# Weight chunks at a cycle of eight distances from the activations, in a one-core hybrid attention block

## The chip, the core and the metric

The kernel runs on one core of one Trainium2 chip. A core has a matrix engine (TensorE, PE in the profile; its weight loads stand apart as PEld), a vector engine (DVE), a scalar engine (ACT), a general engine (POOL) and SyncE (SP), whose queue starts the transfers between main memory and the on-chip memory SBUF. Matrix products land in PSUM. The metric is the device time of one execution of the whole program in microseconds (us), as a median over runs.

## The reference

One layer of a transformer block on a sequence of 256 tokens of width 2048, in float32: a half-step gated feed-forward net, attention with two groups of eight heads, an output projection, and a second half-step feed-forward net. Scales, shifts and gates come from a vector `c` through the large matrix `w_ada`.

```python
mod = jax.nn.silu(c) @ w_ada[l] + b_ada[l]
sh1, sc1, gt1, sh2, sc2, gt2, sh3, sc3, gt3 = jnp.split(mod, N_MOD, axis=-1)
f = swiglu(modulate(rms_norm(h, g_ffn1[l]), sh1, sc1), w1_gate[l], w1_up[l], w1_down[l])
h = h + 0.5 * gt1[:, None, :] * f
nrm = modulate(rms_norm(h, g_mix[l]), sh2, sc2)
q, k, v = jnp.split(nrm @ w_qkv[l], 3, axis=-1)
...
mix = jnp.concatenate([o_na, o_dil], axis=-1) @ w_o[l]
h = h + gt2[:, None, :] * mix
f = swiglu(modulate(rms_norm(h, g_ffn2[l]), sh3, sc3), w2_gate[l], w2_up[l], w2_down[l])
h = h + 0.5 * gt3[:, None, :] * f
```

The hidden width of the feed-forward nets is 5632. The q and k of each head are normalised with gains: one pair of gains for the first eight heads, another for the last eight.

## The kernel before

**Pairs of matmuls.** Weights and activations are kept in float32 accuracy by splitting each into a high part (type float32r) and a low part, the rest. `mm2` (lines 153 to 157) multiplies one 128x128 weight block with one activation tile in two matmuls: the high weights with the 512 columns "high and low activation" (line 156), then the low weights with the 256 columns of the high activation alone (line 157). In a matmul of this kind the weights are the stationary operand, loaded by an LDWEIGHTS, and the activations stream past. There are 4384 such pairs: 800 in the up-projection's first part (`pa`), 1920 in the rest of it (`pb`), 1408 in the down-projections (`pd`) and 256 in the output projection (`pso`). The q, k, v projection goes the other way round (`mm3`, line 162): the activations are stationary and the weights stream, three matmuls of 512 columns for each product, 1152 in all.

**Chunks.** All weights come as chunks of 128x1024 (512 KB, eight blocks), in the order in which they are used, listed in `srcs`. The class `W` keeps the stream: `chunk` fetches up to three chunks ahead (`AHEAD`), and for each calls `wraw` (a transfer on SP's queue into one of five `rw` buffers) and `wsplit` (lines 145 to 152): ACT copies the chunk to `hiw` (line 150), DVE subtracts it to get `low` (line 151). `hiw` and `low` have four buffers each (`LOB`), used in turn. The very first 12 chunks (`w1_s`) are used whole, without a split. Between the chunks, at a rate that `pace` sets, the stream also issues a 1 MB transfer of a `w_ada` row block and a reduction of it on DVE (line 131).

**Where tiles lie.** The pools give out addresses in the order of the first request. The activation tiles that stream in `mm2` are `nx` (normalised input), `hd` (hidden) and `ox` (attention output), each 2 KB per partition. In `wsplit` a pad `far` of 192 bytes is requested between the first `hiw` and the first `low`. In the built program every `hiw` buffer starts 64 bytes after an `nx`, `hd` or `ox` tile, counted modulo 256, and every `low` buffer starts at 0 (blocks within a chunk are 512 bytes apart). "The distance 64 and 0" below means this pair of numbers. In the q, k, v projection the same buffers give 64 for the high and 0 for the low weights.

**Order.** A scheduler orders the instructions of each engine by dependencies, except PE's in the attention stage, which are kept in the written order (`manual_schedule`). In that stage the work is cut in units of one chunk each; `at(u, fn)` puts a piece of the attention behind unit `u`. `qk_norm` multiplies q and k by their row factors and by the gains in `gq` (line 543), loaded once for all four gain rows (line 501).

The stages in order of time: start and first norm (0 to 68 us), up-projection of the first net (68 to 408), its down-projection and remaining parts (408 to 800), q, k, v with attention and the output projection (800 to 1226), the second net in the same order (up to 1580, down and the remaining parts to the end).

Of the kernel before, what the change touches and what calls it, by code (L numbers as in the profile page):

```python
# [9 lines left out]
F32 = mybir.dt.float32  # L10
F32R = mybir.dt.float32r
AF = mybir.ActivationFunctionType
ALU = mybir.AluOpType
AX = mybir.AxisListType

P = 128
# [6 lines left out]
HD = 128  # L23
EPS = 1e-6
NEG = -1e30
CW = 1024
# [21 lines left out]
LOB = 4  # L48
URGENT = 400
LINE = 16  # L50
MANUAL = {mybir.EngineType.PE}


# [10 lines left out]
def build(tc, a):  # L64
    nc = tc.nc
    with ExitStack() as ctx:
        cp = ctx.enter_context(tc.tile_pool(name="cp", bufs=1))
        wp = ctx.enter_context(tc.tile_pool(name="wp", bufs=2))
# [35 lines left out]
        cb = cp.tile([P, D], F32, name="cb")  # L104
        mods = [cp.tile([P, KT], F32, tag=f"m{j}", name=f"m{j}") for j in range(9)]
        nx = [cp.tile([P, 2, S], F32R, tag=f"nx{k}", name=f"nx{k}") for k in range(KT)]

        wide = {}
        turn = [0]
# [28 lines left out]
        def wraw(src):  # L138
            raw = wp.tile([P, CW], F32, tag="raw", bufs=RAWB, name="rw")
            nc.sync.dma_start(raw, src)  # L140
            return raw

        far = []

        def wsplit(raw):
            hi = wp.tile([P, CW], F32R, tag="whi", bufs=LOB, name="hiw")
            if not far:
                far.append(wp.tile([P, 3 * LINE], F32, tag="far", bufs=1, name="far"))
            lo = wp.tile([P, CW], F32R, tag="wlo", bufs=LOB, name="low")
            nc.scalar.copy(hi, raw)  # L150
            nc.vector.tensor_tensor(lo, raw, hi.bitcast(F32), ALU.subtract)  # L151
            return hi, lo
# [88 lines left out]
        def bg_use():  # L241
            raw, i, then = pend.pop(0)
            ada_use(raw, i)
            if then:
                then()

        def bg_step():
            i, then = bg.pop(0)
            while len(pend) >= (ARA + ARX - 1 if wide else ARA - 1):
                bg_use()  # L250
            pend.append((ada_issue(i), i, then))
# [9 lines left out]
        def ax_open():  # L261
            wide["cm"] = tc.tile_pool(name="ax", bufs=ARX)
            wide["p"] = wide["cm"].__enter__()
# [7 lines left out]
        srcs = []  # L271
        first = {}
        for nm in ("w1_s", "w1_a", "w1_b", "w1_d", "w1_c", "w1_e", "w_qkv", "w_o",
                   "w2_a", "w2_b", "w2_d", "w2_c", "w2_e"):
            first[nm] = len(srcs)
            srcs += [a[nm][c] for c in range(a[nm].shape[0])]

        class W:
            def __init__(self):
# [6 lines left out]

            def fetch(self, n):
                while self.head < n:
                    self.ready[self.head] = wraw(srcs[self.head])
                    self.head += 1  # L290

            def whole(self):
# [2 lines left out]

            def chunk(self, ahead=AHEAD):
                while self.head <= min(self.tail + ahead, len(srcs) - 1):
                    self.ready[self.head] = wsplit(wraw(srcs[self.head]))
                    self.head += 1
                    self.credit += self.rate  # L300
                    while self.credit >= 1.0 and (bg or pend):
                        self.credit -= 1.0
                        if bg:
                            bg_step()
                        else:
                            bg_use()
                self.tail += 1
                return self.ready.pop(self.tail - 1)
# [100 lines left out]
        hp = hps.enter_context(tc.tile_pool(name="hid1", bufs=F1 + 4))  # L409
        hp.tile([P, LINE], F32, tag="pad", bufs=1, name="pad1")  # L410
        ax_open()
# [36 lines left out]
        for k in range(K1):  # L448
            ws.fetch(2 * k + 2)
            bg_until((KT - 1 - k) * 2)  # L450
            for j in range(2):
                w = ws.whole()
                for b in range(8):
                    f, q = 4 * j + b // 2, b % 2
# [42 lines left out]
        hps.close()  # L497

        with tc.tile_pool(name="att", bufs=2) as ap_, tc.tile_pool(name="atc", bufs=1) as ac:
            gq = ac.tile([P, 4, HD], F32, name="gq")  # L500
            nc.sync.dma_start(gq, a["qkg"].partition_broadcast(P))
            rope = ac.tile([P, 2, 2, 32], F32, name="rope")
            nc.sync.dma_start(rope, a["rope"])
            lnc = ac.tile([P, 2, S], F32, name="lnc")
# [18 lines left out]
            def at(u, fn):  # L523
                slots.setdefault(u, []).append(fn)
# [12 lines left out]
                s_["rr"] = rstd_from(s_["ss"], HD, 8, "rq")  # L537

            def qk_norm(g, j, nm, ps, t, s_):
                gi = j + (0 if g < 2 else 2)  # L540
                xn = ap_.tile([P, 4, HD], F32, tag=f"{nm}n{t}", bufs=1, name=f"{nm}n{t}")
                for i in range(4):
                    nc.vector.scalar_tensor_tensor(
                        xn[:, i, :], ps[t][:, i * P : (i + 1) * P],
                        s_["rr"][:, t * 4 + i : t * 4 + i + 1], gq[:, gi, :], ALU.mult, ALU.mult)
                if g >= 2:
                    ra = ap_.tile([P, 4, 32], F32, tag="ra", bufs=1, name="ra")
                    rb = ap_.tile([P, 4, 32], F32, tag="rb", bufs=1, name="rb")
                    cs = rope[:, t, 0, :].unsqueeze(1).broadcast_to([P, 4, 32])
                    sn = rope[:, t, 1, :]  # L550
                    nc.vector.tensor_tensor(ra, xn[:, :, 0:32], cs, ALU.mult)
                    nc.vector.tensor_tensor(
                        rb[:, :, 0:16], xn[:, :, 16:32],
                        sn[:, 0:16].unsqueeze(1).broadcast_to([P, 4, 16]), ALU.mult)
                    nc.vector.tensor_tensor(
                        rb[:, :, 16:32], xn[:, :, 0:16],
                        sn[:, 16:32].unsqueeze(1).broadcast_to([P, 4, 16]), ALU.mult)
                    nc.vector.tensor_tensor(xn[:, :, 0:32], ra, rb, ALU.add)
                res[g, nm, t] = xn
# [7 lines left out]
            def qkv_unit(u, g, j, nm, cch, st_):  # L567
                def go(whi, wlo):
                    if cch == 0:
                        st_["ps"] = [bank(f"pq{nm}{t}") for t in range(2)]  # L570
                    ps = st_["ps"]
                    for kk in range(2):
                        k = cch * 2 + kk
                        sl = slice(kk * 512, (kk + 1) * 512)
                        for t in range(2):
                            ts_ = slice(t * P, (t + 1) * P)
                            mm3(ps[t], nx[k][:, 0, ts_], nx[k][:, 1, ts_], whi[:, sl], wlo[:, sl],
                                k == 0, k == KT - 1)
                    if cch == 7:
                        if j == 2:  # L580
                            for t in range(2):
                                at(u + 1 + t, lambda t=t: v_split(g, ps, t))
                        else:
                            at(u + 1, lambda: qk_squares(nm, ps, st_))
                            at(u + 2, lambda: qk_rstd(st_))
                            for t in range(2):
                                at(u + 3 + t // QS, lambda t=t: qk_norm(g, j, nm, ps, t, st_))
                return go
# [27 lines left out]
            def head(g, i, a0, b0, c0, d0):  # L616
# [70 lines left out]
                def fetch():  # L687
                    s_["bias"] = na_bias(hd) if g < 2 else lnc

                at(max(0, a0 - 2), fetch)  # L690
                for u, fn in ((a0, a_pe), (a0 + 1, a_ew), (b0, b_pe), (b0 + 1, b_ew1), (b0 + 2, b_ew2),
                              (c0, c_pe), (c0 + 1, c_ew), (d0, d_pe), (d0 + (0 if d0 == LAST else 1), d_ew)):
                    at(u, fn)
# [3 lines left out]
            for g in range(4):  # L697
                for j, nm in ((2, "v"), (1, "k"), (0, "q")):
                    st_ = {}
                    for cch in range(8):  # L700
                        units.append(qkv_unit(len(units), g, j, nm, cch, st_))
            LAST = len(units) + KT - 1
            for b in range(2):
                for d in range(KT):
                    units.append(wo_unit(len(units), b, d))
            ws.pace(RQ)
            with tc.manual_schedule(engines=MANUAL):
                for u in range(len(units)):
# [19 lines left out]
        hp = ctx.enter_context(tc.tile_pool(name="hid2", bufs=F1 + 4))  # L728
        hp.tile([P, LINE], F32, tag="pad", bufs=1, name="pad2")
        ax_open()  # L730
# [104 lines left out]
def _program():  # L835
    import concourse.bacc as _bacc

    nc = _bacc.Bacc("TRN2", target_bir_lowering=False, num_devices=1, dynamic_dma_scratch_size=1024)
    aps = {k: nc.dram_tensor(f"in_{k}_dram", s, F32, kind="ExternalInput").ap() for k, s in _SHAPES.items()}
    aps["out"] = nc.dram_tensor("out_0_dram", (KT, P, S), F32, kind="ExternalOutput").ap()  # L840
    with tile.TileContext(nc) as tc:
        build(tc, aps)
    return nc
# [10 lines left out]
```

## Time and profile before

| | |
|---|---|
| median of 3 runs | 1954.19 us (1942.38 to 1956.5) |
| profiled execution, its own time | 1967.14 us |
| its span | 1965.4 us |
| PE busy, weight loads busy | 1923.0 us (98%), 1659.7 us (84%) |
| DVE busy, ACT busy | 1570.2 us (80%), 906.5 us (46%) |
| mean granted TensorE clock | 0.992 |
| read from main memory | 500.09 MB, mean 256 GB/s |

How to read it: matmuls are pipelined, so that the end of one lies over the start of the next; a busy PE is therefore not a PE at its best. What counts is the time from the start of one matmul to the start of the next. In a group of matmuls that follow each other without a break, it is the stretch divided by their number.

### The profile page before, as it was taken

What the parts mean: (1) busy time and instruction counts of PE and PEld (TensorE: products, weight loads), DVE (VectorE), ACT (ScalarE), POOL (GpSimd) and SP (SyncE); (2) the same over time, 40 slices, a digit from 0 to 9 for tenths busy, and PEclk for the clock granted to TensorE, in tenths of its full rate; (3) what the DMA queues carried; (4) which work ended last, traced back from release to release, by engine and by line L of the source; (5) the groups of instructions that cost most, each with busy time, mean ns of one, the idle gap of its engine ahead of it and who ended that gap; (6) DMA issues with size and microseconds to landing.
All of it is one profiled execution on the core that took longest, in us unless ns stands there. A gap on an engine that the chain in (4) does not pass through costs nothing.

```text
span 1965.4 us, 27570 instructions
## 1 busy us (share of the span) xinstructions
PE 1923.0 (98%) x10564; PEld 1659.7 (84%) x10564; DVE 1570.2 (80%) x2122; ACT 906.5 (46%) x1333; POOL 0.7 (0%) x6
## 2 busy tenths in 40 slices
PE   7999999999999999999999999999999999999999
PEld 5878888888887888887888788888888888888888
DVE  7799999998888867989766799988899865555565
ACT  2444544443333454545554555544455443334442
POOL 0000000000000000000000000000000000000000
PEclk8999999999999999999999999999999999999999
DMA  9988888899998976698655445899976666666664
GB/s 383 360 323 296 310 304 306 301 314 337 350 336 322 330 238 202 206 336 306 219 163 165 152 134 170 317 317 334 324 263 191 192 186 189 187 188 188 188 199 133
DMA packets 120083, 503.98 MB, mean 256 GB/s; under 512 B 13328, under 2 KB 15632, under 8 KB 101520
## 3 DMA queue, kind: packets, MB, share of 16 engines
q1 hardware_dynamic: 119952, 502.24, 75.2%
q8 instruction: 82, 1.34, 0.3%
q14 instruction: 49, 0.40, 0.1%
HBM read 500.09 MB, written 2.10 MB: 256 GB/s over the span
## 4 chain that ended last, share of the span: by engine, by line
PE 86%; DVE 7%; DMA 3%; issue 2%; ACT 2%; SPq 0%; DVEq 0%; ACTq 0%
PE pb L156 22%; PE pd L156 15%; PE pb L157 11%; PE pa L156 9%; PE pd L157 7%; PE pqv L162 5%; PE pa L157 5%; PE pqk L162 4%; DVE low L151 3%; PE pa L455 2%; PE pqq L162 2%; DMA ra<-in_w_ada_dram 2%; PE pso L156 2%; DVE ra L131 1%; DMA rx<-in_w_ada_dram 1%
## 5 line engine op out<-in xcount | busy, mean ns | idle before, releaser
L150 ACT CAST hiw<-rw 128x1024 fp32r<-128x1024 f32 x644 | 674.6, 1051 | 793.3 <-PE pd L156 272.0
L151 DVE TENSOR_TENSOR low<-rw,hiw 128x1024 fp32r<-128x1024 f32 x644 | 783.2, 1222 | 246.3 <-ACT hiw L150 243.5
L156 PE MATMUL pb<-nx,hiw 128*128 128x512 f32 x1920 | 676.4, 395 | 0.0
L157 PE MATMUL pb<-nx,low 128*128 128x256 f32 x1920 | 540.1, 281 | 5.3 <-DVE low L151 5.2
L156 PE MATMUL pd<-hd,hiw 128*128 128x512 f32 x1408 | 489.9, 393 | 0.0
L156 PEld LDWEIGHTS pb<-nx,hiw 128*128 128x128 f32 x1920 | 361.1, 188 | 84.7
L157 PE MATMUL pd<-hd,low 128*128 128x256 f32 x1408 | 393.8, 280 | 1.3 <-DVE low L151 1.3
L157 PEld LDWEIGHTS pb<-nx,low 128*128 128x128 f32 x1920 | 363.0, 189 | 6.3 <-DVE low L151 6.3
L156 PEld LDWEIGHTS pd<-hd,hiw 128*128 128x128 f32 x1408 | 264.3, 188 | 59.0
L156 PE MATMUL pa<-nx,hiw 128*128 128x512 f32 x800 | 283.4, 398 | 3.6 <-ACT hiw L150 3.3
L131 DVE CUSTOM_DVE_ANT_0 ra<-ra,cb,vec 128x2048 f32<-128x2048 f32 x101 | 237.2, 2348 | 43.6 <-DMA ra<-in_w_ada_dram 42.9
L157 PEld LDWEIGHTS pd<-hd,low 128*128 128x128 f32 x1408 | 265.8, 189 | 2.2 <-DVE low L151 2.2
L157 PE MATMUL pa<-nx,low 128*128 128x256 f32 x800 | 225.4, 284 | 3.9 <-DVE low L151 3.8
L156 PEld LDWEIGHTS pa<-nx,hiw 128*128 128x128 f32 x800 | 151.1, 190 | 38.9 <-ACT hiw L150 5.2
L157 PEld LDWEIGHTS pa<-nx,low 128*128 128x128 f32 x800 | 153.0, 191 | 8.5 <-DVE low L151 7.5
L131 DVE CUSTOM_DVE_ANT_0 rx<-rx,cb,vec 128x2048 f32<-128x2048 f32 x43 | 101.0, 2348 | 20.3 <-DMA rx<-in_w_ada_dram 20.2
L156 PE MATMUL pso<-ox,hiw 128*128 128x512 f32 x256 | 92.2, 403 | 0.0
L162 PE MATMUL pqk<-hiw,nx 128*128 128x512 f32 x256 | 85.6, 399 | 0.0
L162 PE MATMUL pqq<-hiw,nx 128*128 128x512 f32 x256 | 84.4, 399 | 0.0
L162 PE MATMUL pqv<-hiw,nx 128*128 128x512 f32 x256 | 82.8, 398 | 0.3 <-ACT nx L225 0.3
L370 DVE SCALAR_TENSOR_TENSOR h<-pd,m,h 128x256 f32<-128x256 f32 x128 | 61.3, 482 | 22.5 <-PE pd L157 20.5
L157 PE MATMUL pso<-ox,low 128*128 128x256 f32 x256 | 72.1, 282 | 0.0
(133 smaller groups left out, 1513.0 us busy)
## 6 DMA issues: line engine op xcount, KB each, us to landing
ra<-in_w_ada_dram SPq DMA_DIRECT2D x101, 1024.0 KB, 7.8
rw<-in_w_b_dram SPq DMA_DIRECT2D x144, 512.0 KB, 4.7
rw<-in_w_d_dram SPq DMA_DIRECT2D x128, 512.0 KB, 4.5
rw<-in_w_a_dram SPq DMA_DIRECT2D x100, 512.0 KB, 5.0
rw<-in_w_c_dram SPq DMA_DIRECT2D x96, 512.0 KB, 4.5
rw<-in_w_qkv_dram SPq DMA_DIRECT2D x96, 512.0 KB, 4.1
rx<-in_w_ada_dram SPq DMA_DIRECT2D x43, 1024.0 KB, 7.6
rw<-in_w_e_dram SPq DMA_DIRECT2D x48, 512.0 KB, 4.2
```

The lines of the kernel that those rows point to most:

```text
L131: held(nc.vector.tensor_tensor_reduce(out=raw, in0=raw, in1=cb, scale=1.0, scalar=vec[:, BA + i : BA + i + 1], op0=ALU.mult, op1=ALU.add, ...
L150: nc.scalar.copy(hi, raw)
L151: nc.vector.tensor_tensor(lo, raw, hi.bitcast(F32), ALU.subtract)
L156: nc.tensor.matmul(out, lh, r, start=first, stop=False)
L157: nc.tensor.matmul(out[:, :S], ll, r[:, 0, :], start=False, stop=last)
L162: nc.tensor.matmul(out, l, r, start=first and i == 0, stop=last and i == 2, **kw)
L370: nc.vector.scalar_tensor_tensor(h[d], part_, g, h[d], ALU.mult, ALU.add)
L455: nc.tensor.matmul(pa[f][:, q, :], w[:, b * P : (b + 1) * P], full[k], start=k == 0 and q == 0, stop=k == K1 - 1 and q == 1, skip_group_ch ...
```

## The change

Each chunk gets a place, a pair of offsets in floats for its high and its low part. `hiw` and `low` become 64 floats longer, and the chunk lies in them at its offset. A new pad of 192 bytes behind `nx` and the loss of `far` bring the start of every `hiw` and every `low` to 0 modulo 256 from the activations, so that the offset in bytes is the distance. By the number of the chunk modulo 8, high and low lie at 48 and 144 bytes, three times at 64 and 0, at 176 and 160, three times at 192 and 0. With a stream that has four buffers in turn, the two pairs called "odd" in the title (48/144 and 176/160) always fall in the first buffer. The chunks of q, k, v lie at 0 and 0. The stationary first 12 chunks, which are not split, move to 0 from 64.

So that the longer tiles find room, the gains are loaded in two halves into one buffer: the first half at the start of the attention stage, the second at unit 56, between the last use of the first half (unit 51) and the first use of the second (unit 66).

```diff
+PLACE = ((12, 36),) + 3 * ((16, 0),) + ((44, 40),) + 3 * ((48, 0),)
...
         nx = [cp.tile([P, 2, S], F32R, tag=f"nx{k}", name=f"nx{k}") for k in range(KT)]
+        cp.tile([P, 3 * LINE], F32, name="pad")
...
-        far = []
-
-        def wsplit(raw):
-            hi = wp.tile([P, CW], F32R, tag="whi", bufs=LOB, name="hiw")
-            if not far:
-                far.append(wp.tile([P, 3 * LINE], F32, tag="far", bufs=1, name="far"))
-            lo = wp.tile([P, CW], F32R, tag="wlo", bufs=LOB, name="low")
+        def wsplit(raw, place):
+            hi = wp.tile([P, CW + 64], F32R, tag="whi", bufs=LOB, name="hiw")[:, place[0] : place[0] + CW]
+            lo = wp.tile([P, CW + 64], F32R, tag="wlo", bufs=LOB, name="low")[:, place[1] : place[1] + CW]
             nc.scalar.copy(hi, raw)
             nc.vector.tensor_tensor(lo, raw, hi.bitcast(F32), ALU.subtract)
             return hi, lo
...
             first[nm] = len(srcs)
-            srcs += [a[nm][c] for c in range(a[nm].shape[0])]
+            for c in range(a[nm].shape[0]):
+                srcs.append((a[nm][c], (0, 0) if nm == "w_qkv" else PLACE[len(srcs) % len(PLACE)]))
...
-                    self.ready[self.head] = wsplit(wraw(srcs[self.head]))
+                    self.ready[self.head] = wsplit(wraw(srcs[self.head][0]), srcs[self.head][1])
...
-            gq = ac.tile([P, 4, HD], F32, name="gq")
-            nc.sync.dma_start(gq, a["qkg"].partition_broadcast(P))
+            gains = {}
+
+            def gain_load(b):
+                gains["t"] = ac.tile([P, 2, HD], F32, tag="gq", name=f"gq{b}")
+                nc.sync.dma_start(gains["t"], a["qkg"][2 * b : 2 * b + 2].partition_broadcast(P))
+
+            gain_load(0)
...
-                gi = j + (0 if g < 2 else 2)
...
-                        s_["rr"][:, t * 4 + i : t * 4 + i + 1], gq[:, gi, :], ALU.mult, ALU.mult)
+                        s_["rr"][:, t * 4 + i : t * 4 + i + 1], gains["t"][:, j, :], ALU.mult, ALU.mult)
...
             LAST = len(units) + KT - 1
+            at(56, lambda: gain_load(1))
```

PE, ACT and POOL have the same instructions in the same order as before. Two queues differ. The first is SP's, at the second half of the attention stage; `rw` are weight chunks, `nab` a bias tile. Before:

```order
L125 DMA ra_11407<-in_w_ada_dram 128x2048
L140 DMA rw<-in_w_qkv_dram 128x1024 x11
L511 DMA nab_8691<-in_nab_dram 128x512
L140 DMA rw<-in_w_qkv_dram 128x1024 x4
L511 DMA nab_8813<-in_nab_dram 128x512
```

And of the changed kernel, at the same place:

```order
L127 DMA ra_11409<-in_w_ada_dram 128x2048
L142 DMA rw<-in_w_qkv_dram 128x1024 x8
L503 DMA gq_8619<-in_qkg_dram 128x256
L142 DMA rw<-in_w_qkv_dram 128x1024 x3
L515 DMA nab_8693<-in_nab_dram 128x512
```

One transfer, the second half of the gains, stands between the eighth and the ninth of eleven chunks.

The second is DVE's, where the first group's q is normalised (`qn`, with the row factors `rqr`) between subtractions for coming chunks (`low`). Before:

```order
L543 SCALAR_TENSOR_TENSOR qn_7726<-pqq_7454,rqr,gq 128x128 x2
L543 SCALAR_TENSOR_TENSOR qn_7752<-pqq_7455,rqr,gq 128x128 x2
L151 TENSOR_TENSOR low<-rw,hiw 128x1024
L543 SCALAR_TENSOR_TENSOR qn_7752<-pqq_7455,rqr,gq 128x128 x2
L131 ISA ra_7738,m_94<-ra_7738,cb,vec 128x2048
```

And of the changed kernel:

```order
L546 SCALAR_TENSOR_TENSOR qn_7726<-pqq_7454,rqr,gq_7106 128x128 x2
L546 SCALAR_TENSOR_TENSOR qn_7752<-pqq_7455,rqr,gq_7106 128x128 x3
L149 TENSOR_TENSOR low<-rw,hiw 128x1024
L546 SCALAR_TENSOR_TENSOR qn_7752<-pqq_7455,rqr,gq_7106 128x128
L133 ISA ra_7738,m_94<-ra_7738,cb,vec 128x2048
```

One subtraction stands one short instruction later; two others, ahead of these rows (one in the norm before the attention, one in the rows just above), move by a few places in the same way.

More of the change, by code (lines that the diff above doesn't have):

```diff
@@ L288, in fetch @@
                 while self.head < n:
-                    self.ready[self.head] = wraw(srcs[self.head])
+                    self.ready[self.head] = wraw(srcs[self.head][0])
                     self.head += 1
```

## Prediction

> **What bounds the kernel now.** I read the page first, then the stretches by stage, then single matmuls in the timeline, and last the waits.
>
> ```profile
> span 1965.4 us, 27570 instructions
> ...
> PE 1923.0 (98%) x10564; PEld 1659.7 (84%) x10564; DVE 1570.2 (80%) x2122; ACT 906.5 (46%) x1333; POOL 0.7 (0%) x6
> ...
> L156 PE MATMUL pb<-nx,hiw 128*128 128x512 f32 x1920 | 676.4, 395 | 0.0
> ...
> L156 PE MATMUL pd<-hd,hiw 128*128 128x512 f32 x1408 | 489.9, 393 | 0.0
> ...
> L156 PE MATMUL pa<-nx,hiw 128*128 128x512 f32 x800 | 283.4, 398 | 3.6 <-ACT hiw L150 3.3
> ...
> L156 PE MATMUL pso<-ox,hiw 128*128 128x512 f32 x256 | 92.2, 403 | 0.0
> ```
>
> PE is the bound: 98% of the span, and its groups show next to no idle time. One matmul of line 156 lasts longer than the time to the next one, so the busy time of such a group, divided by its count, is the time of a pair: 352 ns for `pb`, 348 for `pd`, 354 for `pa`. These are means. The stretches by stage, without the places where stages meet, show what they are means of (columns: length, PE with its count of matmuls, weight loads, DVE, ACT, POOL, granted clock, DMA share, GB/s):
>
> ```profile
> 190.00:400.00 210.00, 210.00 (x1191) 182.66 (x1190) 199.49 (x268) 99.80 (x135) 0.00 (x0) 1.00 0.87 305
> 455.00:595.00 140.00, 140.00 (x826) 124.01 (x825) 114.74 (x119) 54.59 (x52) 0.00 (x0) 1.00 0.93 341
> 610.00:790.00 180.00, 180.00 (x1021) 156.54 (x1020) 140.72 (x177) 86.75 (x114) 0.00 (x0) 1.00 0.78 268
> 1170.00:1210.00 40.00, 40.00 (x237) 35.38 (x236) 37.69 (x69) 24.89 (x44) 0.00 (x0) 1.00 0.57 174
> 1240.00:1400.00 160.00, 160.00 (x916) 140.59 (x915) 142.63 (x155) 77.66 (x94) 0.00 (x0) 1.00 0.91 323
> 1430.00:1580.00 150.00, 150.00 (x859) 132.01 (x858) 138.17 (x201) 76.11 (x110) 0.00 (x0) 1.00 0.68 208
> 1600.00:1760.00 160.00, 160.00 (x916) 140.74 (x915) 83.51 (x87) 59.81 (x58) 0.00 (x0) 1.00 0.63 188
> 1780.00:1890.00 110.00, 110.00 (x630) 96.61 (x629) 64.60 (x79) 52.49 (x70) 0.00 (x0) 1.00 0.62 188
> ```
>
> PE is busy without a break and the clock is full in all eight. Twice the length over the count gives the pair: 353, 339, 353, 338, 349, 349, 349, 349 ns; a stretch cuts a pair or two at its edges, so the true values are about 353, 340 and 350. These are three distinct rates of the same work at the same distances (64 and 0), and neither the tile (`pb`, `pd`, `pa`, `pso`) nor the DMA load decides between them: `pd` runs at 340 in the second row and at 350 in the seventh, and the fast second row has the highest DMA share. The timeline shows how a rate begins:
>
> ```profile
> 451.55 0.40 PE L156 MATMUL pd<-hd,hiw 128*128 128x512 f32 x1
> 451.79 0.28 PE L157 MATMUL pd<-hd,low 128*128 128x256 f32 x1
> 451.91 0.40 PE L156 MATMUL pd<-hd,hiw 128*128 128x512 f32 x1
> 452.64 0.39 PE L157 MATMUL pd<-hd,low 128*128 128x256 f32 x1 [0.34 <-DVE low L151]
> 452.86 0.40 PE L156 MATMUL pd<-hd,hiw 128*128 128x512 f32 x1
> 453.09 0.28 PE L157 MATMUL pd<-hd,low 128*128 128x256 f32 x1
> 453.21 0.39 PE L156 MATMUL pd<-hd,hiw 128*128 128x512 f32 x1
> 453.44 0.28 PE L157 MATMUL pd<-hd,low 128*128 128x256 f32 x1
> 453.55 0.39 PE L156 MATMUL pd<-hd,hiw 128*128 128x512 f32 x1
> ```
>
> A pair takes 0.36 us just before one short wait (451.55 to 451.91) and 0.34 us after it (453.21 to 453.55), and the second row of the stretches shows that 0.34 then holds for 140 us. So PE falls into a rhythm, keeps it, and a disturbance may throw it into another. My reading, an inference: the stream of activations and the load of the next weights run side by side, and their relative phase settles where they either don't hinder each other (340) or hinder each other in every pair (350, 353). Rates below 340 appear in no stretch; I take 340 as the floor. The q, k, v matmuls have a rate of their own:
>
> ```profile
> 824.82 22.40 PE pqk L162 x96
> 847.22 22.40 PE pqq L162 x96
> ...
> PE pb L157 <- DVE low L151: 5.2, 2, 4.6
> ...
> PE pa L157 <- DVE low L151: 3.8, 6, 0.8
> ```
>
> 22.40 us over 96 is 233.3 ns for 512 columns. In a 340 pair the high matmul's successor starts 0.23 us after it (453.21 to 453.44) and the low one's 0.11 us after that: 512 and 256 columns share the 340 as two to one, which puts the floor for 512 columns at 226.7 ns. The last two rows are PE's waits for `low` in the up-projections (total, times, longest): 9 us in all.
>
> **The change part by part.** Nothing is taken from PE's work; what can move is the rate.
>
> *The excess now.* The two 353 rows hold (1191 + 1021) / 2 = 1106 pairs, 13.3 ns over the floor: 14.7 us. The four 350 rows hold 1660 pairs, 10 ns over: 16.6 us. The 532 pairs at 340 have none. The remaining 1086 of the 4384 pairs I take at the mean of these, 31.3 us / 3298 = 9.5 ns: 10.3 us. Sum 41 us. The four groups of line 156 bound it above: 1541.9 us less 4384 x 0.34 is 51, with part of the waits and the cold start in it; 31 bounds it below.
>
> *Three of four chunks at 64/0 or 192/0.* At 64/0 the trace shows all three rates. What the odd chunk adds is a disturbance every 32 pairs, so that by this reading a rhythm lasts no longer than 11 us. If what follows an odd chunk is the 340 rhythm, these chunks lose their excess. For 192/0 no row exists; the nearest is 64/0, with the same low distance and a high one that is a multiple of 64 too, so I take 340 for it, with 353 as the other end.
>
> *The odd chunks.* A quarter of 4384, 1096 pairs, at distances no row shows. Ends: 340 and 353.3, all the trace has. I take the middle, 6.7 ns over the floor: 7.3 us (0 to 14.6). A worse value can't be excluded; it is the slow rival's.
>
> *q, k, v at 0 and 0.* 1152 matmuls at 233.3. In the 340 rhythm the high matmul runs at the floor beside the load of low weights at distance 0, the row nearest to this case. So I take the floor: 1152 x 6.7 = 7.7 us gained. The other end is the 353 rhythm, 235.6 for 512 columns: 2.6 us lost.
>
> *What is late next.* A faster PE meets DVE and DMA. In the first stretch DVE is busy 199.5 us; at 340 its 1191 matmuls would take 202.5 us, so DVE would be 98.5% busy, and I let 3 of the 7.9 us come back as waits for `low`. In 1430 to 1580 it would be 95%, and the 1170 row ran at 340 with DVE at 94% without a break: no loss. Before 190 us PE already waits for DVE (the row of `pa` above); of the 10.3 us of the rest I drop 3. DMA delivered 341 GB/s at the 340 rate, more than any other stretch asks.
>
> *Gains in two halves, moved subtractions.*
>
> ```profile
> L501 SPq DMA_DIRECT2D gq<-in_qkg_dram x1: 327/327/327, 795.4 to 795.4; - x1
> ...
> DMA to landing us min/median/max: 4.7/4.7/4.7
> ...
> SPq L140 <- DVE low L151: 1077.8, 474, 10.4
> ```
>
> The second half lands about 4.7 us after its issue and is first used ten units later, some 28 us at 12 matmuls of 233 ns each. Its issue costs SP 0.3 us on a queue that waits 1078 us for free buffers; its wait for the last use of the first half, five units back, is behind the wait that the next chunk's transfer has anyway. The subtractions that change places run three chunks ahead of use. Nothing for both; without that cover it would be one wait of some 5 us.
>
> *Sum.* 41 - 7.3 - 3 - 3 + 7.7 = 35 us off the profiled execution's 1967 us: **1932 us**. That execution is 13 us above the median of the runs shown. The runs' spread (1942 to 1967) is of the size that the rhythms' luck would give, so I read it as such: an execution whose rhythm is forced has no luck, and 35 is taken from 1967, not from 1954. If the 13 us were the price of being profiled, it would be 1919.
>
> **The rivals.** About 1% is what a measurement of this kernel can tell from no change: below 1934.6 is faster, above 1973.7 slower.
>
> *The distance has no say.* The rhythm is drawn by chance after each disturbance, whatever the addresses. For it: one pair of distances shows all three rates, and no row shows a second pair. Against: nothing else in the rows tells the stages apart. The drawn rates would average as now: 1954. The Trainium skill (TensorE: Matmul & The Clock Gate, "Step-by-step: what each phase is for") says that PE reads streamed operand and weights through two independent ports, so that loading the next weights takes nothing from the running matmul; by that rule addresses can't matter and this rival holds. The trace's three rates at a full clock show that something beyond the two ports is in play, but not that it is the address.
>
> *The odd chunks set a bad rhythm, and the rest keeps it.* The place: every chunk after an odd one. The threes settle at 350 (3288 x 10 = 33 us) and the odd chunks, out of step, pay twice the worst excess (1096 x 26.7 = 29 us): 62 against 41 us now, 1988 us; with q, k, v at 0/0 as now. For it: 353 and 350 hold 2766 of 3298 pairs, so the slow rhythms are the commoner ones, and the lucky 140 us at 340 would be lost. Against: a disturbance every 11 us is also a fresh chance. It decides from a mean pair of 11 ns over the floor on.
>
> **How the numbers follow.** Forecast 0.55; its own range is 1918 (odd chunks at the floor, no waits: 1967 - 49) to 1950 (odd chunks at 353, q, k, v at the other end: 1932 + 7.3 + 10.3). Above 1934.6 lies a part of it worth 0.15. No say: 0.22, of it 0.18 within 1%, 0.03 faster, 0.01 slower by luck. Bad rhythm: 0.23, all slower. So faster 0.43, same 0.33, slower 0.24. The range 1917 to 1978 holds the first two and the milder part of the third.
>
> **What would show it.** In the changed profile: pairs of 340 ns in the six chunks at 64/0 and 192/0 of each eight, in all stages alike; another value in every fourth chunk; 21.8 us for 96 matmuls of q and k; the mean of the `pb` and `pd` groups near 342; waits of PE for `low` between 190 and 400 us. Long stretches at 350 or 353 through odd chunks would make the distance meaningless; pairs above 353 in every fourth chunk, with 350 behind them, would be the slow rival; a DVE at 99% with PE waiting outside that stretch would mean that I took the cover for too thick.

## The result, and the profile after

| | before | changed |
|---|---|---|
| median (lowest to highest, runs) | 1955.35 us (1942.38 to 1956.79, 4) | 1929.38 us (1927.8 to 1933.81, 4) |
| ratio, 95% interval | 1 | 0.9876, 0.9831 to 0.9922 |
| profiled execution, its own time | 1967.14 us | 1933.81 us |

The changed kernel is faster by 1.2% (0.8 to 1.7). A second comparison, told with the last experiment, gave 0.9842 (0.9815 to 0.9869). The runs also lie closer together: those before spread over 14 us, with the profiled one over 25, the changed ones over 6.

The page of the changed kernel, the rows that answer to those shown of before:

```profile
span 1932.0 us, 27568 instructions
...
PE 1887.6 (98%) x10564; PEld 1640.8 (85%) x10564; DVE 1565.2 (81%) x2122; ACT 906.7 (47%) x1333; POOL 0.7 (0%) x6
...
L154 PE MATMUL pb<-nx,hiw 128*128 128x512 f32 x1920 | 659.8, 391 | 0.0
...
L154 PE MATMUL pd<-hd,hiw 128*128 128x512 f32 x1408 | 482.7, 391 | 0.0
...
L154 PE MATMUL pa<-nx,hiw 128*128 128x512 f32 x800 | 276.5, 392 | 3.8 <-ACT hiw L148 3.3
...
L154 PE MATMUL pso<-ox,hiw 128*128 128x512 f32 x256 | 92.0, 403 | 0.0
```

Line 156 of before is line 154 here. DVE, ACT and the matmul count stand where they stood; PE's busy time is 35.4 us less. Busy over count gives a pair: `pb` from 352 to 344 ns, `pd` from 348 to 343, `pa` from 354 to 346, `pso` 360 and 359. The stretches by stage (columns as before: length, PE with its count, weight loads, DVE, ACT, POOL, granted clock, DMA share, GB/s):

```profile
190.00:390.00 200.00, 200.00 (x1172) 176.65 (x1171) 194.52 (x264) 99.37 (x133) 0.00 (x0) 1.00 0.89 314
455.00:585.00 130.00, 130.00 (x762) 114.64 (x761) 104.86 (x109) 49.74 (x48) 0.00 (x0) 1.00 0.93 337
610.00:775.00 165.00, 165.00 (x967) 145.63 (x967) 131.05 (x168) 82.82 (x108) 0.00 (x0) 1.00 0.79 272
1230.00:1375.00 145.00, 145.00 (x849) 127.86 (x848) 129.09 (x141) 70.86 (x86) 0.00 (x0) 1.00 0.91 332
1410.00:1560.00 150.00, 150.00 (x878) 132.27 (x878) 141.26 (x207) 77.63 (x114) 0.00 (x0) 1.00 0.68 214
1580.00:1735.00 155.00, 155.00 (x909) 136.95 (x908) 83.67 (x89) 59.74 (x57) 0.00 (x0) 1.00 0.64 192
1755.00:1855.00 100.00, 100.00 (x587) 88.36 (x586) 60.42 (x74) 48.35 (x64) 0.00 (x0) 1.00 0.63 192
```

Twice the length over the count is 341, 341, 341, 342, 342, 341, 341 ns, where the stages of before stood at 353, 340 or 350. All stages now run alike, at the same full clock. The timeline shows the chunks of one cycle; each row is the first high matmul of a chunk at 48/144, of the first of three at 64/0, of the chunk at 176/160 and of the first of three at 192/0:

```profile
244.90 0.39 PE L154 MATMUL pb<-nx,hiw 128*128 128x512 f32 x1
...
247.69 0.39 PE L154 MATMUL pb<-nx,hiw 128*128 128x512 f32 x1
...
255.85 0.39 PE L154 MATMUL pb<-nx,hiw 128*128 128x512 f32 x1
...
258.62 0.39 PE L154 MATMUL pb<-nx,hiw 128*128 128x512 f32 x1
```

A chunk is eight pairs. The 48/144 chunk takes 2.79 us (349 ns a pair), the three at 64/0 8.16 us (340), the one at 176/160 2.77 us (346).

To put sums on this, the steps from one pair's start to the next were counted in the timeline, leaving out steps with a wait or another matmul in them (some 90 of the 4384). The excess over 340 ns, over the pairs counted, is 40.6 us before and 11.1 us after. By distance, before and after:

| distance | mean pair, ns | pairs at 341.5 ns or less |
|---|---|---|
| 64/0, before (all) | 349.4 | 16% |
| 64/0, after | 341.4 | 85% |
| 192/0, after | 340.4 | 93% |
| 176/160, after | 346.7 | |
| 48/144, after | 348.3 | |

A row of the chain of work that ended last, of the changed kernel, and then PE's waits for `low` (total in us, times, longest):

```profile
810.98 21.76 PE pqk L160 x96
```

```profile
PE pb L155 <- DVE low L149: 4.6, 2, 3.9
...
PE pa L155 <- DVE low L149: 3.8, 7, 0.8
...
PE pd L155 <- DVE low L149: 2.5, 3, 1.1
```

The 96 matmuls of k take 21.76 us (226.7 ns each) where they took 22.40; over all 1152 of q, k, v the mean is 228.0 after 233.1 ns, 5.7 us. PE's waits for `low` are 10.9 us in all, after 10.3. The steps behind a matmul of the pairs or of q, k, v that are 30 ns or more over its floor hold 35.7 us, after 33.8. So 29.5 us come from the pairs, 5.7 from q, k, v, and 1.9 go back into waits: 33.3 us, and the two profiled executions differ by 33.3.

### The profile page after: what moved, and what is told of

The parts are those of the page before. It is cut to its first block, busy times and chain, and to the rows that moved or that the text cites. A ratio compares the mean times of both kernels' runs of the same rounds, so it can differ in the third digit from the quotient of the medians.

```text
span 1932.0 us, 27568 instructions
## 1 busy us (share of the span) xinstructions
PE 1887.6 (98%) x10564; PEld 1640.8 (85%) x10564; DVE 1565.2 (81%) x2122; ACT 906.7 (47%) x1333; POOL 0.7 (0%) x6
## 4 chain that ended last, share of the span: by engine, by line
PE 86%; DVE 7%; DMA 3%; issue 2%; ACT 2%; SPq 0%; DVEq 0%; ACTq 0%
PE pb L154 22%; PE pd L154 15%; PE pb L155 11%; PE pa L154 8%; PE pd L155 8%; PE pa L155 4%; PE pqk L160 4%; PE pqv L160 4%; DVE low L149 3%; PE pqq L160 3%; PE pa L454 2%; DMA ra<-in_w_ada_dram 2%; PE pso L154 2%; DVE ra L133 1%; ACT hiw L148 1%
## 5 line engine op out<-in xcount | busy, mean ns | idle before, releaser
L154 PE MATMUL pb<-nx,hiw 128*128 128x512 f32 x1920 | 659.8, 391 | 0.0
L155 PE MATMUL pb<-nx,low 128*128 128x256 f32 x1920 | 533.5, 278 | 4.6 <-DVE low L149 4.6
L154 PE MATMUL pd<-hd,hiw 128*128 128x512 f32 x1408 | 482.7, 391 | 0.0
L154 PE MATMUL pa<-nx,hiw 128*128 128x512 f32 x800 | 276.5, 392 | 3.8 <-ACT hiw L148 3.3
```

The lines of the kernel that those rows point to most:

```text
L154: nc.tensor.matmul(out, lh, r, start=first, stop=False)
L155: nc.tensor.matmul(out[:, :S], ll, r[:, 0, :], start=False, stop=last)
```

## The experiments

The theory on test: the odd chunks let the pairs find the 340 rhythm again, and the distances decide it. The rivals: the calmer distance 192/0 does it without odd chunks; any disturbance now and then would do; any odd distance would do; only one of the two odd ones does. All kernels are the changed one with another `PLACE` and little else, so that the tiles, pads and gain halves stay. "Excess" is again the time of the counted pairs over 340 ns, from the starts in the profiled execution; in the kernel before it was 40.6 us.

### One part alone: the buffers, and q, k, v

All chunks at 64/0, q, k, v at 64/0 as well: the change without any new distance.

```diff
-PLACE = ((12, 36),) + 3 * ((16, 0),) + ((44, 40),) + 3 * ((48, 0),)
+PLACE = 8 * ((16, 0),)
...
-                srcs.append((a[nm][c], (0, 0) if nm == "w_qkv" else PLACE[len(srcs) % len(PLACE)]))
+                srcs.append((a[nm][c], (16, 0) if nm == "w_qkv" else PLACE[len(srcs) % len(PLACE)]))
```

> The new layout (longer tiles, new pad, gains in two halves), but every chunk, those of q, k, v too, at 64 and 0 as before the change. If the distance sets the rhythm: as the kernel before, 1955 us with its spread (1942 to 1967), pairs of 340, 350 and 353 ns in long stretches, q, k, v at 233.3 ns for 512 columns. If the gain came from the rest of the change (the layout of other tiles, the gains in halves): about 1930. If the distance has no say: anything from 1930 to 1955, by chance.

Measured: 1956.59 us (1934.86 to 1961.49, 10 runs), ratio 0.9981 (0.9951 to 1.0012). The pads, the longer tiles and the two halves of the gains cost and bring nothing that shows. Mean pair 347.2 ns, excess 31.0 us.

The same with q, k, v at 0/0:

```diff
-PLACE = ((12, 36),) + 3 * ((16, 0),) + ((44, 40),) + 3 * ((48, 0),)
+PLACE = 8 * ((16, 0),)
```

> Feed-forward nets and output projection at 64 and 0 throughout, q, k, v at 0 and 0. If the distance sets the rhythm: 226.7 ns for a matmul of q, k, v, so some 7.7 us under the kernel with everything at 64 and 0, that is about 1947, with that kernel's spread. If the distance has no say: 233.3 ns stays, 1955.

Measured: 1955.06 us (1952.7 to 1963.4, 10 runs), ratio 0.9995 (0.9974 to 1.0015). The same row of the chain, first with all at 64/0:

```profile
814.05 22.40 PE pqk L160 x96
```

and with q, k, v at 0/0:

```profile
816.16 21.76 PE pqk L160 x96
```

The rate came as expected, 233.3 to 226.7 ns for 512 columns by the distance alone. The time did not follow it: the pairs of this execution, whose distances are the same in both kernels, held an excess of 36.5 us against 31.0. A gain of 5.7 us is lost in the spread that the pairs' rhythms make by themselves. One run in ten of the first kernel came to 1934.86, so luck alone can reach nearly as far as the whole change.

### Without odd chunks

```diff
-PLACE = ((12, 36),) + 3 * ((16, 0),) + ((44, 40),) + 3 * ((48, 0),)
+PLACE = 4 * ((16, 0),) + 4 * ((48, 0),)
```

> No odd chunks: four chunks at 64 and 0, four at 192 and 0, q, k, v at 0 and 0. My theory (the odd chunk brings a phase of its own and hands over a good one): long stretches at 350 or 353 remain, about 1945, as with q, k, v alone. Rival (any change of distance is a fresh draw): mixed rhythms of 11 us each, mean pair about 346, 1940. Rival (64 and 192 in turn are enough, the odd chunks only cost): 340 everywhere, 1923.

Measured: 1950.58 us (1926.44 to 1955.27, 10 runs), ratio 0.9945 (0.9903 to 0.9988). The stretches of this kernel, in the second net's up-projection and its down-projection:

```profile
1420.00:1575.00 155.00, 155.00 (x888) 135.89 (x887) 141.12 (x205) 78.19 (x114) 0.00 (x0) 1.00 0.63 203
1595.00:1750.00 155.00, 155.00 (x888) 135.96 (x887) 82.62 (x88) 58.05 (x56) 0.00 (x0) 1.00 0.61 188
```

Both are 349 ns a pair, as before the change. At 64/0 the mean is 349.6 ns, at 192/0 348.3, excess 38.7 us: 192/0 has the slow rhythms too, and to change between 64/0 and 192/0 does not end them (a chunk at 350 ahead of a step to 192/0 was followed by one at 340 in 1 case of 48). Yet three of the ten runs took 1926.44, 1928.31 and 1932.17 us, as little as the changed kernel, where no run of before lies under 1940. No trace of these three was kept; an execution that once finds the 340 rhythm may keep it at these distances. So the threes alone reach the whole gain in some executions and miss it in most; what the odd chunks add is that it comes every time.

### Only odd distances

```diff
-PLACE = ((12, 36),) + 3 * ((16, 0),) + ((44, 40),) + 3 * ((48, 0),)
+PLACE = 8 * ((12, 36),)
```

> Every chunk of the pairs at 48 and 144, q, k, v at 0 and 0. My theory: each pair costs what the odd chunks show in the changed kernel, about 346.5 ns in one steady rhythm: 4384 x 6.5 = 28 us over the floor against the changed kernel's 11, so about 1947, with little spread. If the distance has no say: 1930, or 340 to 353 in stretches.

Measured: 1959.87 us (1955.39 to 1962.37, 10 runs), ratio 1.0011 (0.9988 to 1.0034). Mean pair 349.8 ns, where one steady 346.5 was expected; excess 42.5 us. There are two rates: of the chunks without a wait 142 run at 347 ns a pair and 359 at 351. 48/144 is no good distance in itself. What it does for its neighbours is the next question.

### One odd chunk among 64/0

48/144 once in eight chunks:

```diff
-PLACE = ((12, 36),) + 3 * ((16, 0),) + ((44, 40),) + 3 * ((48, 0),)
+PLACE = ((12, 36),) + 7 * ((16, 0),)
```

> One chunk of eight at 48 and 144, the other seven at 64 and 0, q, k, v at 0 and 0. My theory (the odd chunk hands over a good phase, which then holds at a constant distance until something disturbs it): the odd chunks' excess halves, from some 8 us to 4, so about 0.2% under the changed kernel, a ratio of about 0.985 to the kernel before; the 64/0 pairs at 340. Rival (the good phase wears off within a few chunks): part of the seven at 350, ratio 0.990 or more. Rival (192/0 is needed): long stretches at 350, ratio 0.995.

Measured: 1942.36 us (1927.84 to 1949.33, 4 runs), ratio 0.9899 (0.9848 to 0.995). And once in four, as dense as the odd chunks of the change:

```diff
-PLACE = ((12, 36),) + 3 * ((16, 0),) + ((44, 40),) + 3 * ((48, 0),)
+PLACE = ((12, 36),) + 3 * ((16, 0),)
```

> One chunk of four at 48 and 144, three at 64 and 0; neither 176/160 nor 192/0. My theory: as the changed kernel, ratio about 0.988 (48/144 costs 1.6 ns a pair more than 176/160, together 1 us). Rival (the two halves of the cycle need each other): 350 in part of the threes, ratio 0.993 or more.

Measured: 1950.33 us (1935.45 to 1953.08, 5 runs), ratio 0.9938 (0.9904 to 0.9972). The theory that any odd chunk resets the rhythm falls here: twice as many odd chunks are not better, and a good part of the gain is missing in both. The excess is 31.1 us in the first and 32.9 in the second, where the two kernels without odd chunks had 31.0 and 36.5. The timeline of the second kernel shows why; the rows are the first high matmuls of a chunk at 64/0, of one at 48/144, of the next at 64/0, and of the one after that:

```profile
1751.26 0.39 PE L154 MATMUL pb<-nx,hiw 128*128 128x512 f32 x1
...
1754.06 0.39 PE L154 MATMUL pb<-nx,hiw 128*128 128x512 f32 x1
...
1756.86 0.40 PE L154 MATMUL pb<-nx,hiw 128*128 128x512 f32 x1
...
1759.67 0.39 PE L154 MATMUL pb<-nx,hiw 128*128 128x512 f32 x1
```

Each takes 2.80 to 2.81 us: 350 ns into the odd chunk, 350 out of it. Over both kernels 350 came out as 350 in 124 of 124 cases; 353 came out as 340 in 3 of 3, and 340 was kept in 56 of 57, which leaves room for the smaller gain.

### A disturbance without a new distance

All chunks at 64/0, and ahead of the first pair of a sum a matmul of 32 columns more, at most once in 32 pairs (128 in all; its result is overwritten):

```diff
-PLACE = ((12, 36),) + 3 * ((16, 0),) + ((44, 40),) + 3 * ((48, 0),)
+PLACE = 8 * ((16, 0),)
...
+        since = [0]
+
         def mm2(out, lh, ll, r, first, last):
+            since[0] += 1
+            if first and since[0] >= 32:
+                since[0] = 0
+                nc.tensor.matmul(out[:, :32], lh, r[:, 0, :32], start=True, stop=True)
```

> No odd chunks: all pairs at 64 and 0, q, k, v at 0 and 0, but an extra matmul of 32 columns ahead of the first pair of a sum, at least 32 pairs apart (128 in all; its result is overwritten). A disturbance without a change of distance. The extra matmuls cost some 60 to 110 ns each, 8 to 14 us. Rival (any disturbance is a fresh draw): a mix of 340, 350 and 353 in stretches of 32 to 40 pairs, near half of the pairs at 340. My theory (what counts is the phase that is handed over, and an extra matmul hands over one fixed phase, good or bad): nearly all at one rhythm after each extra matmul; if it is a bad one, ratio about 1.00.

Measured: 1954.98 us (1953.35 to 1958.76, 10 runs), ratio 0.9988 (0.9963 to 1.0012). An extra matmul of 32 columns starts 28 ns (median) before the pair it precedes, and costs some 110 ns (median, against the same pairs of the kernel without it), 14 us in all. It does change the rhythm, but to either side: from 350 it led to 340 in about half of 81 cases, from 340 to a slower rhythm in 38 of 41. Mean pair 346.8 ns, 33% of the pairs at the floor.

That is not chance, though it looks so in a count. Seven extra matmuls in a row, 32 pairs apart:

```profile
1599.44 0.18 PE L158 MATMUL pd<-hd,hiw 128*128 128x32 f32 x1
...
1610.44 0.18 PE L158 MATMUL pd<-hd,hiw 128*128 128x32 f32 x1
...
1621.75 0.18 PE L158 MATMUL pd<-hd,hiw 128*128 128x32 f32 x1
...
1633.06 0.18 PE L158 MATMUL pd<-hd,hiw 128*128 128x32 f32 x1
...
1644.06 0.18 PE L158 MATMUL pd<-hd,hiw 128*128 128x32 f32 x1
...
1655.37 0.18 PE L158 MATMUL pd<-hd,hiw 128*128 128x32 f32 x1
...
1666.68 0.18 PE L158 MATMUL pd<-hd,hiw 128*128 128x32 f32 x1
```

They lie 11.00, 11.31, 11.31, 11.00, 11.31 and 11.31 us apart: one stretch at 340, two at 350, and again. From 200 us on, where no wait came between, 104 of 105 stretches have the rhythm of the third one before. So the extra matmul is neither a repair nor a fresh draw, and it doesn't hand over one fixed phase either, as the theory had it: it moves the rhythm on by one in a fixed order of three, 340, 350, 350. Without its own 14 us such a kernel would come to about 1941 us, an estimate, and still not to the changed one's time, since two thirds of its pairs are slow.

### Thinner cycles, and 176/160 alone

One odd chunk in eight, of both kinds:

```diff
-PLACE = ((12, 36),) + 3 * ((16, 0),) + ((44, 40),) + 3 * ((48, 0),)
+PLACE = ((12, 36),) + 7 * ((16, 0),) + ((44, 40),) + 7 * ((48, 0),)
```

> A cycle of sixteen: 48/144, seven at 64/0, 176/160, seven at 192/0; q, k, v at 0 and 0. My theory: as one of eight with 64/0, a little better, since 176/160 costs less than 48/144: ratio about 0.985. Rival (the phase wears off sooner at one of the two distances): 350 in the second half of the seven at 64/0 or at 192/0.

Measured: 1928.08 us (1926.34 to 1934.45, 4 runs), ratio 0.9842 (0.9816 to 0.9868); 64/0 341.1, 192/0 340.2 ns, excess 6.4 us. So the gain is back as soon as 176/160 and 192/0 are. 176/160 as the only odd distance, first among 192/0:

```diff
-PLACE = ((12, 36),) + 3 * ((16, 0),) + ((44, 40),) + 3 * ((48, 0),)
+PLACE = ((44, 40),) + 7 * ((48, 0),)
```

> One chunk of eight at 176 and 160, seven at 192 and 0; no 64/0 and no 48/144; q, k, v at 0 and 0. In the runs so far a chunk at 176/160 that comes from 64/0 and goes over into 192/0 always handed over the 340 rhythm, from a slow one too. Theory (the repair lies in 176/160 before 192/0, wherever it comes from): 340 in nearly all chunks at 192/0, as with the cycle of sixteen, ratio about 0.984. Rival (it needs the change from 64 to 192 across the odd chunk): slow rhythms stay slow through 176/160 as they do through 48/144 among 64/0, ratio 0.990 to 0.997.

Measured: 1927.21 us (1926.06 to 1928.13, 4 runs), ratio 0.9845 (0.9812 to 0.9878); 192/0 340.5, 176/160 347.2 ns, excess 5.8 us. Then among 64/0:

```diff
-PLACE = ((12, 36),) + 3 * ((16, 0),) + ((44, 40),) + 3 * ((48, 0),)
+PLACE = ((44, 40),) + 7 * ((16, 0),)
```

> One chunk of eight at 176 and 160, seven at 64 and 0; q, k, v at 0 and 0. Theory (176/160 leaves a phase that is good for whatever follows): 340 in nearly all, ratio about 0.984. Rival (the repair lies in the pair 176/160 and 192/0, or in the change of distance across it): slow stretches go on through the odd chunks, ratio 0.990 to 0.997.

Measured: 1928.79 us (1926.94 to 1929.07, 4 runs), ratio 0.985 (0.981 to 0.989); 64/0 342.0 ns, 81% at the floor, excess 11.3 us. Here is the repair itself, in the timeline of the kernel with 192/0: first high matmuls of a 192/0 chunk, of the 176/160 chunk, of the next 192/0 chunk, of its third pair, and of the pair eight further on:

```profile
1307.93 0.40 PE L154 MATMUL pa<-nx,hiw 128*128 128x512 f32 x1
...
1310.73 0.40 PE L154 MATMUL pa<-nx,hiw 128*128 128x512 f32 x1
...
1313.56 0.40 PE L154 MATMUL pa<-nx,hiw 128*128 128x512 f32 x1
...
1314.26 0.39 PE L154 MATMUL pa<-nx,hiw 128*128 128x512 f32 x1
...
1316.98 0.39 PE L154 MATMUL pa<-nx,hiw 128*128 128x512 f32 x1
```

The chunk before takes 2.80 us, eight pairs of 350; from two pairs behind the odd chunk on, eight pairs take 2.72 us, 340 each. The odd chunk itself, entered at 350, takes 2.83 us, 354 a pair: 176/160 has two rates, 346 ns in nearly all chunks entered at 340, and 346 or 352 to 354 in those entered at a slower one. The handovers of these kernels, of the changed one and of the next section's, where no wait falls into the chunk named, with the rhythm of the last four pairs before that chunk and of the chunk that follows it:

| what lies between | 350 became 340 | 353 became 340 | 340 stayed 340 |
|---|---|---|---|
| 176/160, from 64/0 to 192/0 | all of 11, 350 and 353 together | | all of 139 |
| 176/160, from 192/0 to 192/0 | 4 of 4 | none seen | 88 of 88 |
| 176/160, from 64/0 to 64/0 | 7 of 7 | 0 of 2 | 51 of 53 |
| 48/144, from 64/0 to 64/0 | 0 of 124 | 3 of 3 | 56 of 57 |
| 48/144, from 192/0 to 64/0 | 0 of 2 | none seen | 152 of 152 |
| nothing, from 192/0 to 64/0 | 0 of 52 | none seen | 7 of 15 |
| nothing, from 64/0 to 192/0 | 1 of 48 | 3 of 14 | 4 of 5 |

So the two odd chunks have different parts. 176/160 repairs. 48/144 repairs only the rare 353, and is a bridge: over it a 340 rhythm comes from 192/0 to 64/0, where without it half are lost.

### Can it be thinner still?

176/160 once in sixteen, all the rest at 192/0, beside the changed kernel on one chip:

```diff
-PLACE = ((12, 36),) + 3 * ((16, 0),) + ((44, 40),) + 3 * ((48, 0),)
+PLACE = ((44, 40),) + 15 * ((48, 0),)
```

> One chunk of sixteen at 176 and 160, fifteen at 192 and 0; q, k, v at 0 and 0. Theory (at 192/0 the good phase holds until a wait of PE breaks it, and 176/160 repairs it): the odd chunks' excess falls from 3.8 us (one of eight) to 1.9, a slow stretch after a wait lasts up to 44 us instead of 22; about 1927, 2 to 4 us under the changed kernel. Rival (the phase wears off beyond seven chunks): 350 in the later chunks of the fifteen, 1935 or more.

> The changed kernel itself once more, beside the cycle of sixteen on the same chip: 1929 to 1931, excess of some 11 us in the pairs, of which 7 to 8 in the odd chunks.

Measured: 1928.57 us (1926.46 to 1931.36, 6 runs), ratio 0.9839 (0.9812 to 0.9867); the changed kernel 1928.84 us (1926.29 to 1931.77, 5 runs), ratio 0.9842 (0.9815 to 0.9869). The 2 to 4 us that were expected did not come, though the excess fell from 10.4 to 4.4 us. The stretch with the most DVE work, in the thin cycle, and behind it its largest wait of PE for DVE:

```profile
190.00:390.00 200.00, 200.00 (x1177) 177.00 (x1176) 195.92 (x266) 100.31 (x134) 0.00 (x0) 1.00 0.89 314
```

```profile
PE pb L155 <- DVE low L149: 6.3, 5, 4.2
```

PE does five matmuls more in the same 200 us than the changed kernel of the first section did, and DVE is at 98%. The steps of 30 ns or more over the floor hold 38.9 us, against 34.3 in the changed kernel beside it: 4.6 of the 6 us are given back as gaps, perhaps to DVE in part, but the wait for it in `pb` is only 0.5 us longer than in that kernel (6.3 and 5.8). The two profiled executions of the changed kernel alone differ by 1.4 us in these steps (35.7 and 34.3) and by 1.2 in that wait (4.6 and 5.8), so where the 4.6 us went is open. No cycle was measurably faster than the changed kernel's; one odd distance and one other do as well as the four distances of the change.

## Why the prediction was right, point by point

**The time.** 1932 us were forecast from the profiled execution, which came to 1933.81, and the median of 1929.38 lies between it and the 1919 that stood for the 13 us being a price of profiling. The reading of these 13 us as luck fits: no changed run lies over 1934, and of the runs of before in all comparisons 60 of 67 lie between 1950 and 1970 (six are lower, one took 3838.11 us). Nor do the experiments show a price of profiling: of their twelve profiled executions five lie under the median of their kernel, six over it and one on it.

**Excess now, 41 us.** Counted, it is 40.6.

**Threes to 340.** They came to 341.4 and 340.4 ns, 2.9 us of excess left where none was taken; for 192/0, which had no row, the choice of the near end was right.

**The odd chunks at 346.7, 7.3 us.** 176/160 has 346.7, 48/144 has 348.3: 547 pairs at 6.7 and 534 at 8.3 ns make 8.1 us. The middle had no row behind it, and that it came so near was luck: each of the two distances has rates of its own, 347 and 351 ns for 48/144 by itself, 346 and up to 354 for 176/160.

**q, k, v, 7.7 us.** 5.7 measured. In undisturbed rows the floor of 226.7 ns is there, but the mean of before was 233.1, not 233.3, and 228.0 after it: 1.5 us of excess stay, in single steps of 230 ns and more.

**Waits, 6 us back.** 1.9 us. DVE in 190 to 390 us was 194.5 of 200 us busy, 97%, and not yet in the way; I took its cover for thinner than it was. The term was too large by 4.1 us, the odd chunks and the threes together too small by 3.7, q, k, v too large by 2.0: errors that nearly cancel.

**Gain halves and moved subtractions, nothing.** The kernel with all distances at 64/0 carries both and is level with before (0.9951 to 1.0012).

**The mechanism.** The step that did not hold as put is "What the odd chunk adds is a disturbance every 32 pairs". A disturbance at most once in 32 pairs was tried by itself and gives 0.9988 with 33% of the pairs at the floor; an odd chunk every 32 pairs, 48/144, gives 0.9938. The gain rests on one of the two odd distances, 176/160, which brought the 350 rhythm to 340 in every handover that was counted, and by the table keeps 340 in 278 of 280. The extra matmul moves the rhythm on in its order of three and so can't hold it at 340. That the prediction came out rests on the "if" behind that step ("If what follows an odd chunk is the 340 rhythm"), taken at better than even odds with no row for it: this part was luck.

**The rivals.** "The distance has no say" fell twice: by q, k, v (233.3 to 226.7 ns with nothing but the distance changed) and by the handovers, where 48/144 and 176/160 at the same place do opposite things. The Trainium skill (TensorE: Matmul & The Clock Gate, "Step-by-step: what each phase is for") says that loading the next weights takes no read bandwidth from the running matmul. If nothing else were in play, by that rule the two q, k, v rates would be one; what makes them two, the load of the next operand or something else, no run here shows. "The odd chunks set a bad rhythm" fell in the changed kernel, but its inner half was sound: a disturbed 340 did go to a slower rhythm in 38 of 41 cases of the extra matmul. With 48/144 as the only odd distance, threes that are at 350 stay there, much as that rival had it, without its second half, since the odd chunks cost 350 and not 367.

## What to carry to other kernels

Where a busy engine shows several distinct rates for the same instruction at the same clock, take it as an excess that can be won without moving any work, count it from the starts of the instructions, and look at where tiles lie before looking at the schedule. Test such a cure for what it does at its edges (what rhythm goes into a group, what comes out), not by mean times alone: two offsets that looked alike in a mean, 346.7 and 348.3 ns, were a repair and a mere bridge. Look at the order of what follows a disturbance before calling it chance: counted, the extra matmul's rhythms were a half-and-half draw; in order of time, a cycle of three. And an effect of 6 us can't be read from medians while the rhythms spread the runs over 25 us, so compare rates in the trace, or fix the rhythm first.

## What the runs showed of the hardware

Pairs of a 512 and a 256 column matmul of this type, back to back at a full granted clock, run at 64/0 at one of three rates, 340.0, 350.0 or 353.3 ns, and hold it over hundreds of pairs without any wait. The place of the weights modulo 256 bytes from the streamed activations decides which rates can be and how one passes into the other: 64/0 and 192/0 have the slow ones and the fast one; 176/160 runs at 346 ns, or at up to 354 where it is entered at a slow rate, and hands on 340 in all but four of the handovers counted; 48/144 runs at 347 to 351 and hands on what it got, except that 353 becomes 340. One extra matmul of 32 columns ahead of a pair at 64/0 moves the rate on in the order 340, 350, 350. Stationary activations with streamed weights take 233.3 ns for 512 columns at 64/0 and 226.7 at 0/0.

That this is the phase between the activations' stream and the load of the next weights remains an inference: it fits that an extra matmul ahead of a pair moves the rate on in a fixed order, but no row shows the phase itself. Nor do the runs tell a distance from the weights' own address: in the built programs the activations lie 96 bytes past a multiple of 256 before and after the change alike, and no experiment moves them. Why 176/160 repairs and 48/144 doesn't is open as well, and so is a constant 192/0 or 176/160, which wasn't tried.
